# Pairs of 256-column products with stationary tokens, issued as one 512-column matmul per half of the tokens

## The chip, the cores and the metric

The kernel runs on one core of a Trainium2 chip. The metric is the device time of one execution in microseconds: the median of three runs of the kernel before is 1721.67 us (1721.51 to 1723.84).

## The reference, cut to what matters

Two transformer stacks of depth two follow each other on 256 tokens of width 1024. Each layer adds a scale, a shift and a gate from a conditioning vector `c`; the products below are the ones that the change touches.

```python
mod = c_act @ ada_w[i] + ada_b[i]                      # 1024 x 9216 (first stack), 1024 x 6144 (second)
h = modulate(rms_norm(x, ln_ffn1[i]), sh1, sc1)
x = x + 0.5 * g1 * ((silu(h @ wg) * (h @ wu)) @ wd)    # feed-forward, F = 2816
q, k, v = split(h @ w_qkv, 3)                          # attention: q and k are normed by head
z = gelu(h @ w_in); u, v = split(z, 2)                 # spatial gating: v is normed over its columns
q, f_pre, i_in, g = split(hmix @ w_in, ...)            # hgrn2: i_in and g are used with tokens on rows
q, k_c, v_c, k_s, v_s, k_w, v_w, gate = split(h @ w_in, ...)   # nsa: v_s and v_w with tokens on rows
a, v = split(hffn @ w_up, 2)                           # conv_ffn: two of eleven pieces of v
```

## The kernel before, in words

There are ten stages: feed-forward (0, 2, 3, 5), attention (1), spatial gating (4), hgrn2 (6), convolutional feed-forward (7, 9) and nsa (8). Every weight is read from HBM in pieces of 1 MB (tile `raw`, four slots) and split for float32 accuracy: ScalarE writes the rounded part `whi`, VectorE the remainder `wlo = raw - whi`. Both have six slots of 1024 columns, taken in program order. The normed tokens are split in the same way into `hhi` and `hlo`. Each product is three matmuls: hi by hi, hi by lo, lo by hi.

Most products keep the weights stationary (`up_t`, 256 tokens moving). Where a result is wanted with tokens on its rows, `up_x` keeps 128 tokens stationary and moves 256 columns of weights. It is called with two column sets. Each half of the tokens then has two chains of 24 matmuls, one for each set, and a PSUM tile takes both halves of one set. Since a chain writes one tile, its matmuls stay in their order: for k = 0 to 7 hi and lo weights with `hhi`, then eight with `hlo`. The down products (`pd`) have 512 columns moving and tokens stationary.

At the end of a stage, `down_rest` finishes the first half of the tokens and then the second; the residual (`gy`, `x`), the squares, a power on GpSimd, the scaled rows `xs`, eight transposes (`xT`), eight `h` and then `hhi`, `hlo` follow for one half after the other. Meanwhile TensorE has the rest of the down products and what the next stage can already do. Apart from stage 0, each stage begins with an `up_x` block.

The order on each engine is not written by hand. The program hands its instructions to `Plan`, which simulates the engines and picks at each step the ready instruction with the smallest number in program order; a tile without a free slot, or a chain whose operand is late in that simulation, lets others go first. What comes out is a fixed order per engine, and on the chip every engine waits at the head of its list. Background steps (the products for `mod`: a 1 MB load and two VectorE instructions `acc` each) are interleaved by `tick()`, called once for each load of weights.

Of the kernel before, what the change touches and what calls it, by code (L numbers as in the profile page):

```python
# [9 lines left out]
F32 = mybir.dt.float32  # L10
# [523 lines left out]
class Model:  # L534
# [370 lines left out]
    def up_x(self, w, cols, new, name):  # L905
# [17 lines left out]
                self.mms(p[:, h], pairs)  # L923
        return ps

    def down_begin(self, nk):
        self.acc_d = [[self.pd([128, 512], "pd") for n in range(2)] for h in range(2)]
        self.pend, self.nk = [], nk
# [49 lines left out]
    def flip_tokens(self, a):  # L978

        pt = self.pu([128, 2, 2, 128], "aT")  # L980
        for j in range(2):
            for h in range(2):
                self.nc.tensor.transpose(pt[:, j, h], a[:, h, 128 * j:128 * j + 128], self.ident)
        return pt.rearrange("p j h q -> p j (h q)")


# [99 lines left out]
    def ffn(self, wg, wu, wd, end, acts=()):  # L1086
        nc = self.nc
        acts = list(acts)
        if not acts:
            pg, pv = self.up_x([wg, wu], [0, 0], self.pu, "pgv")  # L1090
            sg = self.s([128, 2, 256], "sg")
            nc.scalar.activation(sg, pg, AF.Silu)
            a32 = self.s([128, 2, 256], "a32")
            nc.vector.tensor_tensor(a32, pv, sg, op=OP.mult)
            pt = self.flip_tokens(a32)
            hi, lo = self.m([128, 2, 256], "ahi", F32R), self.m([128, 2, 256], "alo", F32R)
            nc.scalar.activation(hi, pt, AF.Copy)
            nc.vector.tensor_tensor(lo, pt, hi.bitcast(F32), op=OP.subtract)
            acts.append((hi, lo))
        for f in range(len(acts), 11):  # L1100
            pg = self.up_t(wg, 256 * f, self.pu, "pg")
            pv = self.up_t(wu, 256 * f, self.pu, "pv")
            sg = self.s([128, 2, 256], "sg")
            nc.scalar.activation(sg, pg, AF.Silu)
            a32 = self.s([128, 2, 256], "a32")
            nc.vector.tensor_tensor(a32, pv, sg, op=OP.mult)
            acts.append(self.act_pair(a32, [128, 2, 256]))
        self.ffn_down(wd, acts, end)
# [8 lines left out]
    def conv_ffn(self, i, wup, wd, end):  # L1117
        nc = self.nc
        acts = []
        for f in range(11):  # L1120
            if f == 0:
                vx = []
                for px in self.up_x(wup, [F, F + 256], self.pu, "px"):
                    vx.append(self.m([128, 2, 256], "vx"))
                    nc.scalar.activation(vx[-1], px, AF.Copy)
            if f < 2:
                pv = self.flip_tokens(vx[f])
            pa = self.up_t(wup, 256 * f, self.pu, "pa")
            if f >= 2:
                pv = self.up_t(wup, F + 256 * f, self.pu, "pv")  # L1130
            y = self.s([128, 2, 256], "y")
            cw = self.convw[i]
            for j in range(2):
                t = 2 * f + j
                nc.scalar.activation(y[:, j], pa[:, j], AF.Identity, scale=cw[:, 44 + t:45 + t],
                                     bias=self.cols2[:, 22 * i + t:22 * i + t + 1])
                nc.vector.scalar_tensor_tensor(y[:, j, 1:], pa[:, j, :255], cw[:, 22 + t:23 + t], y[:, j, 1:],
                                               op0=OP.mult, op1=OP.add)
                nc.vector.scalar_tensor_tensor(y[:, j, 2:], pa[:, j, :254], cw[:, t:t + 1], y[:, j, 2:],
                                               op0=OP.mult, op1=OP.add)  # L1140
            sg = self.s([128, 2, 256], "sg")
            nc.scalar.activation(sg, y, AF.Silu)
            a32 = self.s([128, 2, 256], "a32")
            nc.vector.tensor_tensor(a32, pv, sg, op=OP.mult)
            acts.append(self.act_pair(a32, [128, 2, 256]))
        self.ffn_down(wd, acts, end)
# [58 lines left out]
    def attention(self, end):  # L1205
        nc, a = self.nc, self.a
        w = a["attn_w_qkv"][0]
        acts = []
        for hp in range(4):
            qk = []  # L1210
            pqk = self.up_x(w, [256 * hp, D + 256 * hp], self.pd, "pqk")
            for i, g in ((0, self.qg8), (1, self.cols2[:, 47:48])):
                p = pqk[i]
                pv = p.rearrange("p a (s d) -> p (a s) d", d=64)
                r = self.seg_rstd(pv, 8, 64, "rqk")
                qn = self.m([128, 2, 256], "qn")
                nc.vector.tensor_tensor(qn.rearrange("p a (s d) -> p (a s) d", d=64), pv,
                                        r[:, :, None].to_broadcast([128, 8, 64]), op=OP.mult)
                pt = self.pu([128, 2, 2, 128], "qkT")
                for h in range(2):  # L1220
                    for t in range(2):
                        nc.tensor.transpose(pt[:, h, t], qn[:, t, 128 * h:128 * h + 128], self.ident)
                qt = self.m([128, 2, 256], "qT")
                nc.scalar.activation(qt, pt.rearrange("p h t q -> p h (t q)"), AF.Copy, scale=g)
                qk.append(qt)
            p, = self.up_x(w, [2 * D + 256 * hp], self.pd, "pv")
            v = self.m([128, 2, 256], "v")
            nc.scalar.activation(v, p, AF.Copy)
            acts.append(self.attend(hp, qk[0], qk[1], v))
        self.down_begin(8)  # L1230
        wo = a["attn_w_o"][0]
        for f in range(4):
            hi, lo = acts[f]
            self.down(wo, 2 * f, [(hi[:, j], lo[:, j]) for j in range(2)], SKEW[self.now])
        end()
# [88 lines left out]
    def sgu(self, end):  # L1324
        nc, a = self.nc, self.a
        w = a["sgu_w_in"][0]
        vt = [self.P.tile([128, D], F32, name="vt", tag="xs") for h in range(2)]
        st = [self.small(16, "vst") for h in range(2)]
        pv = []
        for b in range(4):  # L1330
            if b % 2 == 0:
                pv += self.up_x(w, [D + 256 * b, D + 256 * b + 256], self.pd, "pv")
            p = pv[b]
            for h in range(2):
                nc.scalar.activation(vt[h][:, 256 * b:256 * b + 256], p[:, h], AF.Gelu, accum_out=st[h][:, b:b + 1])
        for h in range(2):
            m = st[h]
            nc.vector.tensor_reduce(m[:, 4:5], m[:, 0:4], axis=AX.X, op=OP.add)
            nc.vector.tensor_scalar(m[:, 5:6], m[:, 4:5], 1.0 / D, None, op0=OP.mult)
            nc.vector.tensor_scalar(m[:, 6:7], m[:, 5:6], -1.0 / 32., None, op0=OP.mult)  # L1340
            ss = self.small(4, "vss")
            junk = self.m([128, 512], "junk")
            for c in range(2):
                nc.scalar.activation(junk, vt[h][:, 512 * c:512 * c + 512], AF.Square, scale=1 / 32.,
                                     bias=m[:, 6:7], accum_out=ss[:, c:c + 1])
            r = self.rstd(ss, 2)
            nc.vector.tensor_scalar(vt[h], vt[h], m[:, 5:6], r, op0=OP.subtract, op1=OP.mult)
# [22 lines left out]
        for f in range(4):  # L1370
            hi, lo = acts[f]
# [36 lines left out]
    def hgrn(self, end):  # L1408
# [1 line left out]
        w = a["hg_w_in_2"][0]  # L1410
        acts = []
        for hp in range(4):
            pi, pg = self.up_x(w, [2 * D + 256 * hp, 3 * D + 256 * hp], self.pd, "pig")
            v = self.m([128, 2, 256], "v")
            nc.scalar.activation(v, pi, AF.Copy)
            sg = self.sigmoid(pg, 1.0, "sg")
            nc.vector.tensor_tensor(sg, pg, sg, op=OP.mult)
            pf = self.up_t(w, D + 256 * hp, self.pd, "pf")
            lf = self.sigmoid(pf, 1.0, "lf")
            kk = self.sigmoid(pf, -1.0, "kk")  # L1420
# [120 lines left out]
    def nsa(self, end):  # L1541
        nc, a = self.nc, self.a
        w = a["nsa_w_in_2"][0]
        vs = []
        for p in self.up_x(w, [D + 256 + 512, D + 256 + 1024], self.pd, "pv"):
            v = self.m([128, 2, 256], "v")
            nc.scalar.activation(v, p, AF.Copy)
            vs.append(v)

        self.kt = [self.P.tile([128, 2, 2, 256], F32, name="kt", tag=t) for t in ("accg", "gb")]  # L1550
        for i in range(2):
# [167 lines left out]
    def nsa_group(self, g, t, q, vs, vc, lct, gv):  # L1719
# [67 lines left out]
        with nc.together():  # L1787

            nc.tensor.matmul(o, vc[:, g].rearrange("n e d -> n (e d)"), lct, start=True, stop=False)
            for i in range(last + 1):  # L1790
                br, k = divmod(i, t + 1)
                for e in range(2):
                    nc.tensor.matmul(o[64 * e:64 * e + 64], vs[br][:, k, es], pts[e][br][:, k], start=False, stop=i == last)
        act = self.m([128, 2, 2, 128], "nact", F32R)
        nc.scalar.activation(act[:, 0], o, AF.Copy)
        nc.vector.tensor_tensor(act[:, 1], o, act[:, 0].bitcast(F32), op=OP.subtract)
# [98 lines left out]
```

## Time and profile before

| | |
|---|---|
| median of three runs | 1721.67 us |
| the profiled execution | 1727.68 us |
| its span | 1725.9 us |
| TensorE matmul busy | 97% of the span |
| VectorE, ScalarE busy | 76%, 55% |
| 16 DMA engines | 71.6% |
| mean granted TensorE clock | 0.992 of full speed |

Busy time of TensorE counts overlapping, pipelined matmuls, so that cadence (start to start) and waits are read instead. All durations below come from the profiled execution, which lies 6.0 us above the median.

### The profile page before, as it was taken

What the parts mean: (1) busy time and instruction counts of PE and PEld (TensorE: products, weight loads), DVE (VectorE), ACT (ScalarE), POOL (GpSimd) and SP (SyncE); (2) the same over time, 40 slices, a digit from 0 to 9 for tenths busy, and PEclk for the clock granted to TensorE, in tenths of its full rate; (3) what the DMA queues carried; (4) which work ended last, traced back from release to release, by engine and by line L of the source; (5) the groups of instructions that cost most, each with busy time, mean ns of one, the idle gap of its engine ahead of it and who ended that gap; (6) DMA issues with size and microseconds to landing.
All of it is one profiled execution on the core that took longest, in us unless ns stands there. A gap on an engine that the chain in (4) does not pass through costs nothing.

```text
span 1725.9 us, 30930 instructions
## 1 busy us (share of the span) xinstructions
PE 1681.5 (97%) x12646; PEld 1512.0 (88%) x12646; DVE 1309.6 (76%) x1950; ACT 948.0 (55%) x1581; POOL 64.4 (4%) x60
## 2 busy tenths in 40 slices
PE   7999999999999999999999999999999999999998
PEld 5899779889988999788999879989998887589986
DVE  4778688886777888677877787889897557878754
ACT  4444366654445544364644368877554556766542
POOL 0000012100001000001000000000000000000000
PEclk9999999999999999999999999999999999999999
DMA  9998875668886998676788865357888565247662
GB/s 297 308 332 308 284 236 192 212 218 282 276 311 220 329 316 304 233 234 229 235 274 302 311 222 175 120 173 236 278 291 304 187 198 217 86 160 231 215 212 73
DMA packets 264208, 415.25 MB, mean 241 GB/s; under 512 B 12811, under 2 KB 210294, under 8 KB 263042
## 3 DMA queue, kind: packets, MB, share of 16 engines
q1 hardware_dynamic: 264065, 413.27, 71.6%
q8 instruction: 99, 1.62, 0.4%
q14 instruction: 44, 0.35, 0.1%
HBM read 412.14 MB, written 1.10 MB: 239 GB/s over the span
## 4 chain that ended last, share of the span: by engine, by line
PE 86%; DMA 5%; DVE 4%; ACT 3%; issue 1%; POOL 1%; SPq 0%; DVEq 0%; POOLq 0%; ACTq 0%
PE pd L514 22%; PE pv L514 21%; PE pg L514 12%; PE pa L514 7%; PE pig L514 3%; PE pgv L514 3%; PE pq L514 3%; PE pqk L514 2%; DMA raw<-in_ffn_wd 2%; PE pf L514 1%; DVE wlo L514 1%; PE px L514 1%; DMA raw<-in_ffn_wu 1%; ACT whi L514 1%; PE ada L514 1%
## 5 line engine op out<-in xcount | busy, mean ns | idle before, releaser
L514 ACT ACTIVATE whi<-raw 128x1024 fp32r<-128x1024 f32 x512 | 534.5, 1056 | 549.1 <-PE pd L514 152.2
L514 DVE TENSOR_TENSOR wlo<-raw,whi 128x1024 fp32r<-128x1024 f32 x512 | 616.5, 1220 | 230.1 <-ACT whi L514 227.1
L514 PE MATMUL pv<-hhi,whi 128*128 128x256 f32 x912 | 257.5, 282 | 0.0
L514 PE MATMUL pv<-hlo,whi 128*128 128x256 f32 x912 | 257.2, 282 | 0.0
L514 PE MATMUL pv<-hhi,wlo 128*128 128x256 f32 x912 | 257.0, 282 | 0.0
L514 DVE SCALAR_TENSOR_TENSOR acc<-raw,csil,acc 128x1024 f32<-128x1024 f32 x192 | 245.8, 1280 | 14.3 <-DMA raw<-in_ada_w 11.7
L514 PE MATMUL pd<-whi,ahi 128*128 128x512 f32 x604 | 239.2, 397 | 0.6 <-ACT ahi L514 0.6
L514 PE MATMUL pd<-wlo,ahi 128*128 128x512 f32 x604 | 237.8, 394 | 0.0
L514 PE MATMUL pd<-whi,alo 128*128 128x512 f32 x604 | 237.4, 394 | 0.0
L514 PE MATMUL pg<-hhi,whi 128*128 128x256 f32 x624 | 176.9, 283 | 0.0
L514 PE MATMUL pg<-hhi,wlo 128*128 128x256 f32 x624 | 176.1, 282 | 0.0
L514 PE MATMUL pg<-hlo,whi 128*128 128x256 f32 x624 | 176.0, 282 | 0.0
L514 PEld LDWEIGHTS pv<-hhi,whi 128*128 128x128 f32 x912 | 174.3, 191 | 1.2 <-issue 1.2
L514 PEld LDWEIGHTS pv<-hhi,wlo 128*128 128x128 f32 x912 | 174.4, 191 | 0.0
L514 PEld LDWEIGHTS pv<-hlo,whi 128*128 128x128 f32 x912 | 174.2, 191 | 0.0
L514 PEld LDWEIGHTS pd<-whi,ahi 128*128 128x128 f32 x604 | 113.7, 188 | 30.8 <-issue 5.3
L514 PEld LDWEIGHTS pd<-whi,alo 128*128 128x128 f32 x604 | 113.7, 188 | 25.4 <-DVE alo L514 0.2
L514 PEld LDWEIGHTS pd<-wlo,ahi 128*128 128x128 f32 x604 | 113.7, 188 | 25.2 <-DVE wlo L514 0.9
L514 PEld LDWEIGHTS pg<-hhi,whi 128*128 128x128 f32 x624 | 119.3, 191 | 2.6 <-issue 2.5
L514 PEld LDWEIGHTS pg<-hhi,wlo 128*128 128x128 f32 x624 | 119.3, 191 | 0.0
L514 PEld LDWEIGHTS pg<-hlo,whi 128*128 128x128 f32 x624 | 119.3, 191 | 0.0
L514 PE MATMUL pa<-hhi,whi 128*128 128x256 f32 x352 | 99.6, 283 | 0.0
(358 smaller groups left out, 3096.0 us busy)
## 6 DMA issues: line engine op xcount, KB each, us to landing
raw<-in_ada_w SPq DMA_DIRECT2D x112, 1024.0 KB
raw<-in_ffn_wd SPq DMA_DIRECT2D x44, 1024.0 KB
raw<-in_ffn_w_up SPq DMA_DIRECT2D x44, 1024.0 KB
raw<-in_ffn_wg SPq DMA_DIRECT2D x42, 1024.0 KB
raw<-in_ffn_wu SPq DMA_DIRECT2D x42, 1024.0 KB
raw<-in_ffn_w_down SPq DMA_DIRECT2D x22, 1024.0 KB
raw<-in_hg_w_in SPq DMA_DIRECT2D x16, 1024.0 KB
raw<-in_attn_w_qkv SPq DMA_DIRECT2D x12, 1024.0 KB
```

The costliest lines, as they stand in the source:

```text
L514: f(*[real(v) for v in args], **{k: real(v) for k, v in kw.items()})
```

## The change

A new function `up_w` takes the place of `up_x` in the sixteen calls that have two column sets; the one call with a single set (attention's v) keeps `up_x`. It loads each set in two pieces of 512 KB, by halves of the contraction, side by side into one `raw` tile, and splits it into four parts of two k each, in which both sets stand side by side. Each half of the tokens has one chain of 24 matmuls of 512 columns and a PSUM tile of its own. `tick()` is called after each of the four loads. The consumers work by halves of the tokens instead of by column sets.

```diff
+    def up_w(self, w, cols, new, name):
+        parts = []
+        for i in range(2):
+            raw = self.P.tile([128, 4, 2, 256], F32, name="raw", tag="raw")
+            for j, c0 in enumerate(cols):
+                v = w[j] if isinstance(w, list) else w
+                self.load(raw[:, :, j], v[512 * i:512 * i + 512, c0:c0 + 256].rearrange("(k p) f -> p k f", p=128))
+                self.tick()
+            parts += [self.split(raw[:, 2 * k:2 * k + 2], [128, 2, 2, 256]) for k in range(2)]
+        ps = [None, None]
+        for h in self.halves:
+            hs = slice(128 * h, 128 * h + 128)
+            ps[h] = new([128, 2, 256], name)
+            pairs = []
+            for k in range(8):
+                hi, lo = parts[k // 2]
+                pairs += [(self.hhi[:, k, hs], hi[:, k % 2]), (self.hhi[:, k, hs], lo[:, k % 2])]
+            for k in range(8):
+                pairs.append((self.hlo[:, k, hs], parts[k // 2][0][:, k % 2]))
+            self.mms(ps[h], pairs)
+        return ps
...
-            pg, pv = self.up_x([wg, wu], [0, 0], self.pu, "pgv")
+            ps = self.up_w([wg, wu], [0, 0], self.pu, "pgv")
             sg = self.s([128, 2, 256], "sg")
-            nc.scalar.activation(sg, pg, AF.Silu)
             a32 = self.s([128, 2, 256], "a32")
-            nc.vector.tensor_tensor(a32, pv, sg, op=OP.mult)
-            pt = self.flip_tokens(a32)
+            for h in self.halves:
+                nc.scalar.activation(sg[:, h], ps[h][:, 0], AF.Silu)
+                nc.vector.tensor_tensor(a32[:, h], ps[h][:, 1], sg[:, h], op=OP.mult)
+            pt = self.flip_tokens([a32[:, h] for h in range(2)])
...
-            pi, pg = self.up_x(w, [2 * D + 256 * hp, 3 * D + 256 * hp], self.pd, "pig")
+            pig = self.up_w(w, [2 * D + 256 * hp, 3 * D + 256 * hp], self.pd, "pig")
```

The other calls change alike: attention norms q and k of one half together, spatial gating has four GELU instructions of 512 columns in place of eight of 256, and convolution and nsa copy by halves.

How the order moves is shown at the entry into stage 6, where the block is named `pig`. On TensorE, these rows lead up to the second half's transposes, before the change:

```order
L514 MATMUL pig<-whi,hhi 128x256
L514 MATMUL pig<-wlo,hhi 128x256
L514 MATMUL pig<-whi,hhi 128x256
L514 MATMUL pig<-wlo,hhi 128x256
L514 MATMUL pig<-whi,hhi 128x256
L514 MATMUL pig<-wlo,hhi 128x256
L514 MATMUL pig<-whi,hhi 128x256
L514 MATMUL pig<-wlo,hhi 128x256
L514 MATMUL pig<-whi,hlo 128x256 x7
L514 MATMUL xT<-ident,xs 128x128 x4
L514 MATMUL pig<-whi,hlo 128x256
L514 MATMUL xT<-ident,xs 128x128 x4
```

And this is all that stands between the transposes of the first and the second half after the change:

```order
L514 MATMUL xT<-ident,xs 128x128 x8
L514 MATMUL pig<-whi,hhi 128x512
L514 MATMUL pig<-wlo,hhi 128x512
L514 MATMUL pig<-whi,hhi 128x512
L514 MATMUL pig<-wlo,hhi 128x512
L514 MATMUL pig<-whi,hhi 128x512
L514 MATMUL pig<-wlo,hhi 128x512
L514 MATMUL pig<-whi,hhi 128x512
L514 MATMUL pig<-wlo,hhi 128x512
L514 MATMUL pig<-whi,hhi 128x512
L514 MATMUL xT<-ident,xs 128x128 x8
```

Before, 47 of 96 matmuls stand ahead of the second half's transposes (the same rows go on upwards to the first half's eight `xT`); after, 9 of 48.

On VectorE at the same place, from the first half's last `hlo` on, before the change (`ss`, `x_99` and `xs` are the second half's norm):

```order
L514 TENSOR_TENSOR hlo<-h_10715,hhi 128x4x128
L514 TENSOR_TENSOR xrow<-x_99,raw 128x512
L514 TENSOR_SCALAR ss_10686<-ss_10686 128x1
L514 TENSOR_TENSOR wlo<-raw,whi 128x1024
L514 TENSOR_SCALAR ss_10686<-ss_10686 128x1
L514 SCALAR_TENSOR_TENSOR ss_10686<-ss_10686 128x1
L514 TENSOR_SCALAR x_99<-xrow,ss_10686 128x512 x2
L514 TENSOR_SCALAR xs<-xrow,ss_10686 128x512
L514 TENSOR_TENSOR wlo<-raw,whi 128x1024
L514 CAST hhi<-h_10808 128x2x128
```

And after it:

```order
L514 TENSOR_TENSOR hlo<-h_10307,hhi 128x4x128
L514 TENSOR_SCALAR ss_10269<-ss_10269 128x1 x2
L514 SCALAR_TENSOR_TENSOR ss_10269<-ss_10269 128x1
L514 TENSOR_SCALAR x_99<-xrow,ss_10269 128x512
L514 TENSOR_SCALAR xs<-xrow,ss_10269 128x512
L514 TENSOR_SCALAR x_99<-xrow,ss_10269 128x512
L514 TENSOR_TENSOR wlo<-raw,whi 128x1024 x2
L514 CAST hhi<-h_10358 128x2x128 x2
```

The first `wlo` of the piece before is the block's fourth part; the two of the piece after are its third and fourth, and both stand behind `xs`.

On ScalarE near the end of stage 5, `sums` releases the transposes `modt`, for which TensorE waits. Before (`dhi` are parts of the ninth of eleven loads of the down weights, the two `whi` behind it of the tenth):

```order
L514 ACTIVATE whi<-raw 128x1024 x9
L514 ACTIVATE dhi<-raw 128x512 x4
L514 ACTIVATE whi<-raw 128x1024 x2
L514 ACTIVATE sums<-modc 128x512
L514 ACTIVATE whi<-raw 128x1024 x4
```

After:

```order
L514 ACTIVATE whi<-raw 128x1024 x8
L514 ACTIVATE dhi<-raw 128x512 x2
L514 ACTIVATE sums<-modc 128x512
L514 ACTIVATE dhi<-raw 128x512 x2
L514 ACTIVATE whi<-raw 128x1024 x6
```

`sums` moved from behind the tenth load to the middle of the ninth, and `modc`, which it reads, from behind 192 matmuls of `pd` to behind 144.

## Rows read from the trace of the kernel before

**Rows 1.** The page: span and busy time of the engines
```profile
span 1725.9 us, 30930 instructions
PE 1681.5 (97%) x12646; PEld 1512.0 (88%) x12646; DVE 1309.6 (76%) x1950; ACT 948.0 (55%) x1581; POOL 64.4 (4%) x60
```
**Rows 2.** Chain of waits in order of time (start, us, what): runs of matmuls
```profile
359.90 8.40 PE pgv L514 x70
...
679.55 44.09 PE pd L514 x192
...
755.81 16.68 PE pv L514 x139
...
1177.72 9.35 PE px L514 x78
...
1673.88 38.96 PE pd L514 x168
```
**Rows 3.** Waits of TensorE: who for whom, us in total, times, longest
```profile
PE xT L514 <- DVE xs L514: 9.2, 4, 5.2
PE modt L514 <- ACT sums L514: 3.0, 2, 2.7
...
PE abp L514 <- DMA hankel<-bdram: 2.7, 1, 2.7
```
**Rows 4.** Timeline of the entry into stage 6 (start, us, engine, instruction)
```profile
1022.53 1.03 PE L514 MATMUL xT<-ident,xs 128*128 128x128 f32 x8
...
1027.59 1.21 DVE L514 TENSOR_TENSOR wlo<-raw,whi 128x1024 fp32r<-128x1024 f32 x1
...
1028.18 0.19 ACT L514 ACTIVATION_READ_ACCUMULATOR xs<-xrow 128x1 f32 x1
...
1029.24 0.89 DVE L514 TENSOR_SCALAR x<-xrow,ss 128x512 f32<-128x512 f32 x2
...
1030.04 0.48 DVE L514 TENSOR_SCALAR xs<-xrow,ss 128x512 f32<-128x512 f32 x1
1030.16 0.71 ACT L514 ACTIVATE xs<-xrow,ss 128x512 f32<-128x512 f32 x1
...
1030.60 0.63 PE L514 MATMUL xT<-ident,xs 128*128 128x128 f32 x4
```
**Rows 5.** Chain of waits: last runs of the block at three entries
```profile
557.56 5.01 PE pgv L514 x40
...
832.87 4.75 PE pgv L514 x40
...
1033.58 5.02 PE pig L514 x40
```
**Rows 6.** Timeline of TensorE: first transpose at four other entries
```profile
352.56 0.30 PE L514 MATMUL xT<-ident,xs 128*128 128x128 f32 x1 [2.55 <-DVE xs L514]
...
546.51 0.27 PE L514 MATMUL xT<-ident,xs 128*128 128x128 f32 x1
...
821.70 0.27 PE L514 MATMUL xT<-ident,xs 128*128 128x128 f32 x1
...
1170.75 0.30 PE L514 MATMUL xT<-ident,xs 128*128 128x128 f32 x1 [1.27 <-DVE xs L514]
```
**Rows 7.** The page's costliest groups: VectorE's background step
```profile
L514 DVE SCALAR_TENSOR_TENSOR acc<-raw,csil,acc 128x1024 f32<-128x1024 f32 x192 | 245.8, 1280 | 14.3 <-DMA raw<-in_ada_w 11.7
```
**Rows 8.** Stretches: PE, PEld, DVE, ACT, POOL busy; PEclk, DMA share, GB/s
```profile
225.00:250.00 25.00, 21.55 (x157) 18.61 (x155) 21.95 (x33) 17.17 (x33) 6.57 (x3) 1.00 0.75 236
350.00:375.00 25.00, 21.67 (x172) 21.46 (x172) 20.86 (x33) 17.96 (x35) 1.43 (x2) 0.93 0.51 170
1000.00:1025.00 25.00, 21.70 (x99) 16.69 (x96) 19.68 (x32) 15.02 (x29) 2.02 (x2) 0.93 0.67 215
```
**Rows 9.** Timeline near the end of stage 5
```profile
1002.68 2.00 ACT L514 ACTIVATE whi<-raw 128x1024 fp32r<-128x1024 f32 x2 [2.11 <-DMA raw<-in_ffn_wd]
...
1005.23 0.66 PE L514 MATMUL modt<-ident,sums 128*128 128x128 f32 x4 [2.70 <-ACT sums L514]
```

More of the change, by code (lines that the diff above doesn't have):

```diff
@@ L982, in flip_tokens @@
             for h in range(2):
-                self.nc.tensor.transpose(pt[:, j, h], a[:, h, 128 * j:128 * j + 128], self.ident)
+                self.nc.tensor.transpose(pt[:, j, h], a[h][:, 128 * j:128 * j + 128], self.ident)
         return pt.rearrange("p j h q -> p j (h q)")
@@ L1121, in conv_ffn @@
             if f == 0:
[L1122 to L1125, printed above, removed]
+                px = self.up_w(wup, [F, F + 256], self.pu, "px")
+                vx = [self.m([128, 2, 256], "vx") for h in range(2)]
+                for h in self.halves:
+                    nc.scalar.activation(vx[h], px[h], AF.Copy)
             if f < 2:
-                pv = self.flip_tokens(vx[f])
+                pv = self.flip_tokens([vx[h][:, f] for h in range(2)])
             pa = self.up_t(wup, 256 * f, self.pu, "pa")
@@ L1209, in attention @@
         for hp in range(4):
+            pqk = self.up_w(w, [256 * hp, D + 256 * hp], self.pd, "pqk")
+            qn = [None, None]
+            for t in self.halves:
+                pv = pqk[t].rearrange("p a (s d) -> p (a s) d", d=64)
+                r = self.seg_rstd(pv, 8, 64, "rqk")
+                qn[t] = self.m([128, 2, 256], "qn")
+                nc.vector.tensor_tensor(qn[t].rearrange("p a (s d) -> p (a s) d", d=64), pv,
+                                        r[:, :, None].to_broadcast([128, 8, 64]), op=OP.mult)
             qk = []
-            pqk = self.up_x(w, [256 * hp, D + 256 * hp], self.pd, "pqk")
             for i, g in ((0, self.qg8), (1, self.cols2[:, 47:48])):
[L1213 to L1218, printed above, removed]
                 pt = self.pu([128, 2, 2, 128], "qkT")
-                for h in range(2):
-                    for t in range(2):
-                        nc.tensor.transpose(pt[:, h, t], qn[:, t, 128 * h:128 * h + 128], self.ident)
+                for t in self.halves:
+                    for h in range(2):
+                        nc.tensor.transpose(pt[:, h, t], qn[t][:, i, 128 * h:128 * h + 128], self.ident)
                 qt = self.m([128, 2, 256], "qT")
@@ L1328, in sgu @@
         st = [self.small(16, "vst") for h in range(2)]
[L1329 to L1335, printed above, removed]
+        for b in range(2):
+            pv = self.up_w(w, [D + 512 * b, D + 512 * b + 256], self.pd, "pv")
+            for h in self.halves:
+                nc.scalar.activation(vt[h][:, 512 * b:512 * b + 512], pv[h].rearrange("p a f -> p (a f)"), AF.Gelu,
+                                     accum_out=st[h][:, b:b + 1])
         for h in range(2):
             m = st[h]
-            nc.vector.tensor_reduce(m[:, 4:5], m[:, 0:4], axis=AX.X, op=OP.add)
+            nc.vector.tensor_tensor(m[:, 4:5], m[:, 0:1], m[:, 1:2], op=OP.add)
             nc.vector.tensor_scalar(m[:, 5:6], m[:, 4:5], 1.0 / D, None, op0=OP.mult)
@@ L1412, in hgrn @@
         for hp in range(4):
-            pi, pg = self.up_x(w, [2 * D + 256 * hp, 3 * D + 256 * hp], self.pd, "pig")
+            pig = self.up_w(w, [2 * D + 256 * hp, 3 * D + 256 * hp], self.pd, "pig")
             v = self.m([128, 2, 256], "v")
-            nc.scalar.activation(v, pi, AF.Copy)
-            sg = self.sigmoid(pg, 1.0, "sg")
-            nc.vector.tensor_tensor(sg, pg, sg, op=OP.mult)
+            sg = self.m([128, 2, 256], "sg")
+            for h in self.halves:
+                nc.scalar.activation(v[:, h], pig[h][:, 0], AF.Copy)
+                nc.scalar.activation(sg[:, h], pig[h][:, 1], AF.Sigmoid)
+                nc.vector.tensor_tensor(sg[:, h], pig[h][:, 1], sg[:, h], op=OP.mult)
             pf = self.up_t(w, D + 256 * hp, self.pd, "pf")
@@ L1543, in nsa @@
         w = a["nsa_w_in_2"][0]
[L1544 to L1548, printed above, removed]
+        vs = [self.m([128, 2, 256], "v") for h in range(2)]
+        pv = self.up_w(w, [D + 256 + 512, D + 256 + 1024], self.pd, "pv")
+        for h in self.halves:
+            nc.scalar.activation(vs[h], pv[h], AF.Copy)
         self.kt = [self.P.tile([128, 2, 2, 256], F32, name="kt", tag=t) for t in ("accg", "gb")]
@@ L1792, in nsa_group @@
                 for e in range(2):
-                    nc.tensor.matmul(o[64 * e:64 * e + 64], vs[br][:, k, es], pts[e][br][:, k], start=False, stop=i == last)
+                    nc.tensor.matmul(o[64 * e:64 * e + 64], vs[k][:, br, es], pts[e][br][:, k], start=False, stop=i == last)
         act = self.m([128, 2, 2, 128], "nact", F32R)
```

## The prediction

> **What bounds the kernel now.** I read the page first: TensorE 97% busy with matmuls, VectorE 76%, ScalarE 55% [rows 1]. That share counts overlapping matmuls, so I went to the chain of waits for the cadence, then to TensorE's waits for where it stands idle, then to the timeline of the stage entries. In the chain the reader is to see long unbroken runs of TensorE [rows 2], and in the waits few and short ones: 9.2 us for the scaled rows `xs` at four entries, 3.0 us for `sums`, 2.7 us for one load in attention [rows 3]. So TensorE's list sets the time nearly throughout, and what matters is (a) what one matmul of the list costs and (b) whether the head of the list is ready. The change alters both.
>
> **The cadence.** Blocks of `up_x` run 70 matmuls of 256 columns in 8.40 us, 139 in 16.68 and 78 in 9.35: 287 in 34.43, 120.0 ns each. The down products have the same shape as the new matmul (tokens stationary, 512 columns of split weights moving): 192 in 44.09 and 168 in 38.96, 360 in 83.05, 230.7 ns each [rows 2]. Two of the first cost 240.0 ns, one of the second 230.7: 9.3 ns less. A block falls from 96 to 48 matmuls, so it gains 48 x 9.3 ns = 0.45 us; sixteen blocks gain 7.1 us. The bound on the one side is this, on the other nothing, where the block isn't what its stage waits for.
>
> These rows have 13 ns over 256 columns at 2.4 GHz and 17 ns over 512. The Trainium skill (TensorE: Matmul & The Clock Gate, section Back-to-back issue gap) gives a fixed 2.5 ns for each matmul at any width; a pair would then gain 2.5 ns and the sixteen blocks 1.9 us, an estimate from that page, and my sum would come out 5.2 us later. The measured runs disagree and decide.
>
> **What the block now waits for.** Seven blocks lie inside a stage (three each in attention and hgrn2, one in spatial gating), with other products around them; I take their whole gain: 7 x 0.45 = 3.1 us less. Nine open a stage, and there the order matters. At the end of a stage the down products hold four of six `whi` and `wlo` slots, so two of the block's four parts are split early and two during the norm. Before, the first two are a whole column set: a chain of 24 matmuls, 2.9 us, can run on the first half of the tokens with them alone, and on the second half again. After, the first two are k = 0 to 3 of both sets, and the one chain stops after 8 of 24 (1.8 us); the tenth matmul needs the third part's `wlo`, the fourteenth the fourth part's.
>
> Worked out at the entry into stage 6: the first transposes start at 1022.53, the squares of the second half are read by 1028.37, `xs` ends 2.15 us later on VectorE and 2.50 us later on ScalarE, at 1030.52 and 1030.87 [rows 4]. After, one `whi` less (1.1 us by its neighbours) lies between the first half's `h` and those squares: 1027.3, so `xs` is there at 1029.4 and 1029.8, and the second half's transposes are over at 1030.5. Behind `xs`, VectorE has one `x` (half of 0.89) and then both parts, 1.21 us each [rows 4]: the third is ready at 1031.1, the fourth at 1032.3. The 9 matmuls ahead of those transposes are over by about 1026.6, so TensorE stands for nearly 3 us, then again for the third and fourth part. At 1032.3 there are 13 of 48 matmuls done; 35 x 230.7 ns = 8.1 us bring the block's end to 1040.4. Before, it ends at 1033.58 + 5.02 = 1038.60 [rows 5], with one matmul of `pf` inside. That is 1.8 + 0.1 = 1.9 us later, in place of 0.45 us earlier.
>
> I counted the other entries alike, by the order after and the durations above, from the first transpose [rows 6] to the block's end:
> - Stage 2: between `xs` and the fourth part VectorE has an `acc` (1.28 us [rows 7]), the third part and all of the second half's `hhi` and `hlo`. The fourth part comes 13.0 us after 352.56, 22 matmuls (5.1 us) follow: 18.1 us against 15.7 (368.30 [rows 2]), with two matmuls of `pg` inside; 0.7 us comes back, since one `gy` less stands ahead of the first `xs`, for which TensorE waits 2.55 us there [rows 6]. Together 1.5 us later.
> - Stage 3: the third part before `xs`, the fourth right behind it, 9.2 us after 546.51; 35 matmuls: 17.3 us against 16.1 (562.57 [rows 5]), of which one matmul is another product's. 1.3 us later.
> - Stage 5: both parts behind `xs` and two `acc` more on VectorE's way; the fourth part at 10.0, the end at 18.1 against 15.9 (837.62 [rows 5]). With the first transposes a little late too, 2.4 us later.
> - Stage 7: fourth part at 9.2, end at 17.3 against 16.3 (1187.07 [rows 2]); 0.7 us comes back as in stage 2 (the wait is 1.27 us [rows 6]). 0.2 us later.
> - Stages 1, 4, 8 and 9 have the third part ahead of `hhi`, or other matmuls for the gap. I take 1.2 us gained of their 1.8.
>
> The nine entries together: 1.9 + 1.5 + 1.3 + 2.4 + 0.2 - 1.2 = 6.1 us later, their gain in cadence already inside. With the blocks inside stages: 6.1 - 3.1 = 3.0 us later.
>
> **The clock.** After long idle stretches the granted clock falls to 1.2 GHz for a while: the stretches from 350 and from 1000 us have a mean of 0.93, with waits of 2.55 and 2.70 us in them; that from 225 us has a wait of as long for `hankel` and stays at 1.00 [rows 3, 6, 8, 9]. A mean of 0.93 over 25 us is 0.07 x 25 = 1.75 us of work lost. New idle stretches of 2 to 3 us at stages 2, 5 and 6 put one more such fall on the path, or two; I take one: 1.8 us.
>
> **The rest.** The 512 KB loads are 32 more issues on SP, which has no row in TensorE's waits; with nothing to hide them in they'd be some 0.4 us each. Two more ticks per block bring the background loads forward and end them earlier in each stage: same bytes, same VectorE work. ScalarE and VectorE have a few more, smaller instructions in feed-forward and hgrn2, four fewer GELU in spatial gating; these lie beside matmuls. One place can go either way: `modt` in stage 5. TensorE waits 2.70 us for `sums`, which stands behind a load that came late [rows 9]. After, `sums` needs only the ninth load, not the tenth; but TensorE asks for it 48 matmuls (11.1 us) earlier. Gone with the fall of the clock behind it, this is 4.5 us gained; if the loads come as late as now, it is about as much lost, an estimate. In attention the stall for `hankel` (2.7 us [rows 3]) has 23 + 12 matmuls before it now in place of 25, so up to 2.7 us less, or the same if a background load is put in front of it. I take nothing for both and keep both ends: 7 us down, 5 us up.
>
> Sum: 3.0 + 1.8 = 4.8 us later than the profiled execution's 1727.68 us. That one lies 6.0 us over the median of the runs, and I shift by that: 1721.67 + 4.8 = 1726.5 us.
>
> **Rivals.**
> - The gain stands (faster). If VectorE and ScalarE have the late parts ready before the transposes, all sixteen blocks gain: 1721.67 - 7.1 = 1714.6; with the stall at `modt` gone too, 1710. For it: the long even runs of [rows 2], and PSUM tiles that come free by halves. Against: the order itself, which puts the parts behind `xs` at stages 5, 6 and 7.
> - Gain and loss cancel (no change). The entries lose less, because idle time there was partly spent before (9.2 us for `xs` [rows 3]): entries 3 us later, inside blocks 3 us earlier: 1721.7.
> - The background sums decide (slower by more). `sums` stands behind late loads at the end of stage 5, TensorE stands 6 us in place of 2.7 and falls to the low clock: 4 to 5 us on top of the forecast, 1731. It decides from the point where the ninth load lands later than TensorE's 144th down matmul.
> - The change isn't what it says: no, the list has 48 matmuls of 512 columns a block.
>
> **How the numbers follow.** My forecast has 0.42, the background rival 0.18, no net change 0.20, the full gain 0.20. Its own range is 1724 to 1730. For eight in ten: downwards I stop between the full gain and the forecast's lower end, at 1714.5; upwards at 1735, the background rival with a second fall of the clock. About 0.2%, 3.4 us, is what a measurement of this kernel tells from no change: slower by more takes the forecast and the background rival, 0.58, less what lies near the border, plus a little of the cancelling case: 0.56. Within it 0.23, faster 0.21.
>
> **What would show it.** Right: 230 ns from matmul to matmul inside the blocks; TensorE's waits with `pig`, `pgv` for `wlo`, and `xT` for `xs` longer by several us in all; blocks at stages 2, 3, 5 and 6 that end 17 to 18 us after the first transpose; more stretches below a clock of 1.00 after them. Wrong: those blocks end within 16 us, or the cadence is the gain and the waits are those of before. Then the slot argument fails, or ScalarE and VectorE are faster through the entry than I counted.

## The result, and the profile after

| | before | after |
|---|---|---|
| median | 1722.76 us (4 runs, 1721.51 to 1724.76) | 1733.03 us (4 runs, 1731.33 to 1734.65) |
| ratio, 95% interval | | 1.0051 [1.0036, 1.0066] |
| the profiled execution | 1727.68 us | 1731.33 us |

The change is slower by 0.5%, 6 to 11 us. The prediction had the direction, and 1733.0 lies in its wide range (1714.5 to 1735); but it had about half of the size (1726.5), and the measured time lies above the range of its own forecast (1724 to 1730). The two profiled executions differ by only 3.7 us, because the first trace of before is one of its longer executions; a second trace of before (below) is the better pair.

The page of after has the span and the engines, to lay beside [rows 1]; there are 768 fewer matmuls (16 blocks of 96 became 48), and 8.6 us less of their busy time:

```profile
span 1729.6 us, 29460 instructions
PE 1672.9 (97%) x11878; PEld 1463.5 (85%) x11878; DVE 1310.7 (76%) x1957; ACT 953.3 (55%) x1588; POOL 62.9 (4%) x60
```

The chain of waits of after (start, us, what) has runs inside two blocks and one of the down products:

```profile
1306.06 33.13 PE pd L514 x144
...
1375.41 7.76 PE pv L514 x34
...
1537.38 7.60 PE px L514 x33
```

Inside the blocks a matmul of 512 columns comes every (7.76 + 7.60) / 67 = 229.3 ns. That is the cadence foretold from [rows 2] (230.7). The waits of TensorE in after (us in total, times, longest), to lay beside [rows 3]:

```profile
PE xT L514 <- DVE xs L514: 16.5, 10, 5.1
PE pTc L514 <- DVE lc L514: 6.3, 1, 6.3
PE pgv L514 <- DVE wlo L514: 3.2, 2, 2.0
...
PE abp L514 <- DMA hankel<-bdram: 0.8, 1, 0.8
```

`xs` costs 7.3 us more than in [rows 3], and `pgv` waits 3.2 us for `wlo` where the trace of before has 0.5, as foretold. `modt` is gone. New, and in no part of the prediction, is one wait of 6.3 us in nsa: the transposes `pTc` wait for `lc`, the scores of its compressed branch. The timeline there (start, us, engine, instruction):

```profile
1447.59 1.52 PE L514 MATMUL pcs<-kct,q 128*128 128x32 f32 x12
...
1449.79 3.71 DVE L514 TENSOR_TENSOR wlo<-raw,whi 128x1024 fp32r<-128x1024 f32 x3
1450.07 1.99 ACT L514 ACTIVATE whi<-raw 128x1024 fp32r<-128x1024 f32 x2
...
1452.08 1.28 ACT L514 ACT_TABLE_LOAD   x1
...
1453.88 0.29 ACT L514 ACTIVATE lc<-lc 128x128 f32<-128x128 f32 x1
...
1455.40 1.01 PE L514 MATMUL pTc<-ident,lc 128*32 128x128 f32 x4 [6.29 <-DVE lc L514]
```

`pcs` ends at 1449.1, the exponent of `lc` starts at 1453.88: ScalarE first splits two weights and loads a table, VectorE splits three. The stretches around it (PE, PEld, DVE, ACT, POOL busy; PEclk, DMA share, GB/s) show what follows:

```profile
1028.00:1031.00 3.00, 2.88 (x11) 2.11 (x9) 2.97 (x5) 3.00 (x9) 0.00 (x0) 0.52 0.02 7
1444.00:1451.00 7.00, 5.11 (x41) 3.10 (x39) 5.38 (x19) 4.32 (x8) 0.00 (x0) 1.00 1.02 407
1452.00:1468.00 16.00, 12.60 (x45) 5.48 (x46) 8.41 (x27) 8.45 (x26) 0.00 (x0) 0.50 0.48 172
```

From 1452 on, while TensorE still waits, it has 1.2 GHz, for 16 us. The first of these rows is the other fall, behind the entry into stage 6, where the forecast had put it. That entry, in the timeline of after, to lay beside [rows 4]:

```profile
1021.09 1.03 PE L514 MATMUL xT<-ident,xs 128*128 128x128 f32 x8
...
1024.92 0.40 PE L514 MATMUL pig<-whi,hhi 128*128 128x512 f32 x1
...
1026.92 0.49 DVE L514 TENSOR_SCALAR xs<-xrow,ss 128x512 f32<-128x512 f32 x1
...
1027.46 1.41 PE L514 MATMUL xT<-ident,xs 128*128 128x128 f32 x8 [2.14 <-DVE xs L514]
...
1027.72 2.35 DVE L514 TENSOR_TENSOR wlo<-raw,whi 128x1024 fp32r<-128x1024 f32 x2
...
1028.99 0.80 PE L514 MATMUL pig<-wlo,hhi 128*128 128x512 f32 x1
...
1037.39 2.00 PE L514 MATMUL pig<-whi,hlo 128*128 128x512 f32 x8
```

TensorE stops behind the ninth matmul (1024.92) and waits for `xs`; the two late `wlo` stand behind `xs` on VectorE, and the tenth matmul starts at 1028.99. All as foretold.

### The profile page after: what moved, and what is told of

Its sections match the earlier page's. It is cut to its first block, busy times and chain, and to the rows that moved or that the text cites. A ratio compares the mean times of both kernels' runs of the same rounds, so it can differ in the third digit from the quotient of the medians.

```text
span 1729.6 us, 29460 instructions
## 1 busy us (share of the span) xinstructions
PE 1672.9 (97%) x11878; PEld 1463.5 (85%) x11878; DVE 1310.7 (76%) x1957; ACT 953.3 (55%) x1588; POOL 62.9 (4%) x60
## 5 line engine op out<-in xcount | busy, mean ns | idle before, releaser
L514 DVE SCALAR_TENSOR_TENSOR acc<-raw,csil,acc 128x1024 f32<-128x1024 f32 x192 | 246.0, 1281 | 19.9 <-DMA raw<-in_ada_w 17.1
```

Of the source, the lines that this page charges most:

```text
L514: f(*[real(v) for v in args], **{k: real(v) for k, v in kw.items()})
```

## The experiments

Every kernel is made from the two shown above; the diffs are shortened to the lines that matter, and the first one has its condition written out for one stage. A block that opens a stage is called an opener. "After" and "before" are the changed kernel and the one before it. Medians, ratios and intervals are against before in the same batch (1722.66, 1723.09 and 1723.31 us).

**A second trace of before.**

> The kernel before, unchanged, for a second trace of it: which waits of the first trace are of the order, and which of one execution. With an order that is the same there, the run with the block only inside stages took 195.0 us for stage 5 (200.8 in the first trace) and 155.5 for stage 8 (160.2), each counted from first xT to first xT. If the wait of modt for sums and the two low-clock stretches in stage 8 belong to one execution, this one takes some 195 and 156 us there and the whole 1718 to 1723; if they belong to the order, 200 and 160 again and 1727.

1719.85 us. Without any edit, stage 5 takes 196.5 us (200.8 in the first trace, counted from first `xT` to first `xT`), stage 8 157.1 (160.2); the other stages agree within 0.3. Two stretches, of the second trace, and behind them one of the first for the later place:

```profile
1000.00:1025.00 25.00, 23.90 (x132) 19.55 (x125) 22.27 (x39) 18.53 (x36) 4.02 (x4) 1.00 0.58 179
1500.00:1515.00 15.00, 13.27 (x66) 8.95 (x66) 11.93 (x30) 9.27 (x23) 0.55 (x1) 1.00 0.09 24
```

```profile
1505.00:1520.00 15.00, 13.27 (x52) 8.02 (x52) 9.24 (x25) 7.44 (x21) 0.55 (x1) 0.77 0.00 1
```

So the 2.70 us for `sums` and the fall behind it in [rows 8, 9], and the second fall in stage 8, belong to that execution: 4.3 + 3.1 = 7.4 of the 7.8 us between the two.

Against the second trace, after is 11.5 us longer (spans 1729.6 and 1718.1). Both are short executions of their kernels, 3.5 and 1.7 us under the medians. By stages, worked out from the timelines in the same way (us; "ticks alone" and "two ticks in nsa" are kernels below, "inner" the block inside stages alone, with two ticks):

| stage | before, 2nd | after | two ticks in nsa | ticks alone | inner |
|---|---|---|---|---|---|
| 0 | 216.5 | 217.2 | 217.0 | 216.9 | 217.4 |
| 1 attention | 127.4 | 126.8 | 127.2 | 129.1 | 123.1 |
| 2 | 194.0 | 196.1 | 196.1 | 194.4 | 194.1 |
| 3 | 195.1 | 196.4 | 196.4 | 196.9 | 195.9 |
| 4 spatial gating | 80.1 | 79.7 | 79.7 | 80.3 | 79.8 |
| 5 | 196.5 | 196.8 | 196.7 | 197.8 | 195.8 |
| 6 hgrn2 | 148.3 | 150.9 | 150.9 | 150.0 | 148.5 |
| 7 | 195.1 | 195.5 | 195.5 | 195.8 | 193.8 |
| 8 nsa | 157.1 | 161.9 | 155.8 | 158.5 | 155.4 |
| 9 | 199.8 | 200.2 | 200.6 | 199.7 | 199.9 |

**The block inside stages only.** Attention's and hgrn2's hp = 1 to 3 and spatial gating's second pair call `up_w`, the nine openers keep `up_x` and their consumers.

```diff
+            if hp:
                 pqk = self.up_w(w, [256 * hp, D + 256 * hp], self.pd, "pqk")
+            else:
+                pqk = self.up_x(w, [256 * hp, D + 256 * hp], self.pd, "pqk")
```

> The 512-column block stands only in the seven places inside a stage (three in attention, three in hgrn2, one in spatial gating); the nine blocks that open a stage are those of the kernel before, with their consumers. My theory (cadence gains in every block, the entries give it back and more): 7 x 0.45 = 3.1 us less than before, about 1719.6 where before is 1722.8; waits of xT for xs at stage entries as before (9 us), inner blocks at 230 ns a matmul. Rival A (the loss comes from the four calls of tick and the smaller loads wherever the block stands): 1723 to 1727, no gain, with new waits inside attention or hgrn2. Rival B (cadence isn't a gain on the path): 1722.8.

1717.67 us, 0.9975 [0.9964, 0.9986]: 2.4 to 6.2 us less, which holds the theory's 3.1. So the loss comes with the changed openers; whether by their 512 columns or by their ticks this run doesn't tell.

**The block at the openers only**, the mirror image.

> The mirror image: the 512-column block stands only in the nine places that open a stage, the seven inside a stage are those of the kernel before. Theory: the whole loss and none of the inner gain, 3.1 us over the changed kernel: about 1736, 13 us over before. xT waits 16 us for xs, as in the changed kernel. Rival A (loss spread over all sixteen blocks): between before and the changed kernel, about 1728. Rival B (the inner blocks do not matter): 1733.

1729.47 us, 1.0047 [1.0035, 1.0059]. The 1736 of the theory is missed, and TensorE waits 12.2 us for `xs`, not 16. By the time rival A (1728) is nearest; by the ratios (1.0047, and 1.0051 for after) rival B is: with the openers changed, the inner blocks no longer gain anything. In the traces they still give 0.9 us in hgrn2 and 1.0 in spatial gating, but attention is 3.1 us longer with them and their ticks (126.8 against 123.7).

**Two ticks instead of four.**

```diff
-                self.tick()
+                if j:
+                    self.tick()
```

> The changed kernel with tick called once per raw tile, so twice per block as before, not four times. In the order this puts the third and fourth part's wlo ahead of the second half's xs on VectorE at stages 2 and 7, the third part's at stages 3 and 5, and leaves stages 4, 6, 8 and 9 as they are. Theory (late parts behind xs make the loss, and at these stages the extra background steps push them there): stages 2, 3, 5 and 7 end their blocks 1 to 2 us earlier each, together 5 us less than the changed kernel, about 1728; stage 6 shows the same wait as in the changed kernel. Rival (only the layout by halves of the contraction matters, ticks are nothing): 1733, the same. Third (background work moved later into the stages meets the ends of the stages): 1735 and a wait of modt for sums at the end of stage 5.

1719.39 us, 0.9984 [0.9974, 0.9994]. This one line takes away the whole loss (13.6 us by the medians, 11.5 by the two ratios), far more than I expected, and turns the change into a small gain. The 16.5 us for `xs` and 6.3 for `lc` become:

```profile
PE xT L514 <- DVE xs L514: 11.7, 8, 5.1
...
PE pgv L514 <- DVE wlo L514: 1.9, 2, 1.0
```

`pTc` has no wait any more. The ticks, which the prediction had at nothing, are the suspect.

**The ticks alone, in the kernel before.** Same 256-column chains and loads, one line more:

```diff
             raw = self.w_cols(w[i] if isinstance(w, list) else w, c0, 256)
+            if len(cols) == 2:
+                self.tick()
```

> The kernel before (256-column chains, same loads and parts) with one change: tick is called twice after each load of a block with two column sets, so four times per block as in the changed kernel. In the order this alone puts the late parts' wlo behind xs at the entries into stages 2, 3, 5, 6 and 7, and takes the four background products ada from between pcs and pTc in nsa. Theory as it stands after the run with two ticks (the ticks make the loss, not the 512-column layout): nsa 5 to 6 us longer with a wait of pTc for lc of 6 us, entries 1 us each, 1730 to 1736. Rival (layout by halves of the contraction and the slots make the loss; ticks matter only with them): 1722 to 1725 outside nsa, at most 1728 with it.

1728.38 us, 1.0027 [1.0013, 1.0040], slower by 2.2 to 6.9: between the theory's 1730 and the rival's 1728, so that the time alone decides nothing, and about half of what after loses (1.0051). Its trace has the waits of after without the new block:

```profile
PE xT L514 <- DVE xs L514: 13.5, 6, 5.0
PE pTc L514 <- DVE lc L514: 4.9, 1, 4.9
```

In nsa the theory misses: the wait is there, but the stage is only 1.4 us longer than in the second trace of before, not 5 to 6.

What the entries do, worked out from the timelines: us from the first transpose to the end of the block (start of its last matmul plus the cadence), and in brackets TensorE's wait ahead of that transpose.

| entry | foretold | before, 2nd | after | ticks alone | two ticks |
|---|---|---|---|---|---|
| 1 | | 17.5 | 18.2 | 18.6 | 18.3 |
| 2 | 18.1 | 15.6 (2.6) | 17.5 (0.6) | 15.9 (3.6) | 15.7 (1.3) |
| 3 | 17.3 | 15.9 | 17.2 | 17.8 | 15.8 |
| 4 | | 19.4 | 19.3 | 19.6 | 19.2 |
| 5 | 18.1 | 15.7 | 17.1 | 16.5 | 16.2 |
| 6 | 17.9 | 15.9 | 18.1 | 16.6 | 18.6 |
| 7 | 17.3 | 16.2 (1.3) | 16.3 (2.2) | 16.5 (2.2) | 14.3 (1.3) |
| 8 | | 15.1 | 15.5 | 15.9 | 15.3 |
| 9 | | 15.1 | 15.4 | 15.1 | 15.5 |

With the brackets, after loses 7 us against before at the nine entries, the ticks alone 8, the new block with two ticks 1. A tick brings a background step forward, and its two `acc` of 1.28 us [rows 7] stand on VectorE just where `gy`, `xs` and the late `wlo` queue. At the entry into stage 5 VectorE has this around the second half's `xs`, in the second trace of before:

```profile
826.33 1.22 DVE L514 TENSOR_TENSOR wlo<-raw,whi 128x1024 fp32r<-128x1024 f32 x1
827.99 0.49 DVE L514 TENSOR_SCALAR xs<-x,ss 128x512 f32<-128x512 f32 x1 [0.44 <-POOL ss L514]
828.39 1.28 DVE L514 SCALAR_TENSOR_TENSOR acc<-raw,csil,acc 128x1024 f32<-128x1024 f32 x1
...
830.59 1.22 DVE L514 TENSOR_TENSOR wlo<-raw,whi 128x1024 fp32r<-128x1024 f32 x1
```

And this with the ticks alone, where `acc` has taken the place of a `wlo` ahead of `xs` (after has the same three instructions, from 828.71):

```profile
830.08 1.28 DVE L514 SCALAR_TENSOR_TENSOR acc<-raw,csil,acc 128x1024 f32<-128x1024 f32 x1
831.80 0.49 DVE L514 TENSOR_SCALAR xs<-x,ss 128x512 f32<-128x512 f32 x1 [0.44 <-POOL ss L514]
832.20 2.36 DVE L514 TENSOR_TENSOR wlo<-raw,whi 128x1024 fp32r<-128x1024 f32 x2
```

The ticks aren't all of it: stage 6, which has no background steps of its own, is late by the block itself (18.6 with two ticks).

**Two ticks in nsa only**, the rest as in after:

```diff
-                self.tick()
+                if j or self.now != 8:
+                    self.tick()
```

> The changed kernel with two ticks instead of four in the one block of nsa (stage 8), four everywhere else; layout as changed. In the order the four ada products stand between pcs and pTc again. Theory (half of the loss is this one place: a wait of 6.3 us for lc and 17 us at the low clock instead of 7): stage 8 takes 157 us instead of 161.9, the whole about 1727 to 1728; entries at stages 2, 3, 5, 6 and 7 as in the changed kernel. Rival A (the nsa wait is hidden or comes back later): 1732 to 1733. Rival B (nsa is the whole loss): 1720.

1727.49 us, 1.0020 [1.0007, 1.0033]; stage 8 takes 155.8 us, the entries are those of after. The same place in its timeline:

```profile
1448.13 2.77 PE L514 MATMUL pcs<-kct,q 128*128 128x32 f32 x12
...
1450.82 1.94 PE L514 MATMUL ada<-raw,csil 128*32 128x512 f32 x8
...
1451.27 0.31 ACT L514 ACTIVATE lc<-lc 128x128 f32<-128x128 f32 x1 [1.97 <-DVE lc L514]
...
1452.81 1.01 PE L514 MATMUL pTc<-ident,lc 128*32 128x128 f32 x4
```

Eight background products `ada` fill TensorE between `pcs` and `pTc`, and `lc` goes ahead of the splits. With four ticks the `ada` loads are issued earlier in the stage, their products are done, and weights stand there ready to be split instead. In this trace the low clock is over soon (again PE, PEld, DVE, ACT, POOL; PEclk):

```profile
1449.00:1454.00 5.00, 4.95 (x23) 2.65 (x25) 2.90 (x15) 3.03 (x13) 0.00 (x0) 0.50 0.87 341
1455.00:1471.00 16.00, 16.00 (x121) 12.87 (x121) 10.50 (x28) 9.12 (x23) 0.00 (x0) 1.00 0.32 122
```

The second trace of before has this short fall too:

```profile
1443.00:1449.00 6.00, 5.95 (x21) 1.96 (x20) 4.09 (x18) 4.69 (x12) 0.00 (x0) 0.50 0.98 366
```

So 5.5 us of the loss by the medians (6.1 in the stage) hang on one block's two ticks.

**Other slots for the late parts.** The opener's third and fourth part become eight tiles of 512 columns in the pool of 22 that the activations use:

```diff
+            if i and early:
+                for k in range(4):
+                    hi, lo = self.m([128, 2, 256], "dhi", F32R), self.m([128, 2, 256], "dlo", F32R)
+                    self.split_to(hi, lo, raw[:, k])
```

> The changed kernel with the third and fourth part of each block that opens a stage taken from another pool (eight tiles of 512 columns, 22 slots) in place of the whi and wlo slots that the down products hold; the rest is as changed. In the order 21 of 24 matmuls of the first half stand ahead of the second half's transposes at stage 5 in place of 9, 15 in place of 9 at stages 3 and 6, 10 in place of 9 at stage 2. Theory (slots hold the late parts back): stage 5 gains 2 us, stages 3 and 6 one us each, stage 2 under a half; less 0.2 us for each entry for more, smaller split instructions; 1729 to 1731. Rival (the slots are not what the parts wait for, VectorE and ScalarE are full there): 1733 or later, TensorE's wait for xs as long as in the changed kernel (16 us).

1720.43 us, 0.9995 [0.9982, 1.0008]: more than expected, and not only where expected. Stage 5's block ends at 14.9 (17.1), stage 6's at 16.2 (18.1), stage 2's at 15.7 (17.5), but stage 3's at 18.2 (17.2), at the low clock; attention and nsa are 3 us shorter each, which the theory had not (another order in both; `pTc` still waits 4.9 us). The slots do hold the late parts back, at three of the four entries that were named; how much of the gain is theirs this run doesn't tell.

**Both.**

> The changed kernel with both edits: late parts of each opening block in the other pool, and two ticks per block. Theory 1 (slots and ticks act on the same wait, the parts behind xs): no better than two ticks alone, 1718 to 1720. Theory 2 (they add): 1715 to 1717. The small splits of 512 columns cost some 0.2 us per entry of VectorE and ScalarE, so 1721 is possible where that lies on the path.

1715.54 us, 0.9951 [0.9937, 0.9965]: more than either alone, as theory 2 has it. If they added in full, 0.9984 less the 0.0056 that the slots gave with four ticks would be 0.9928, an estimate with an interval of its own; they add in good part.

**And the chain in another order.**

```diff
-            for k in range(8):
-                pairs += [(self.hhi[:, k, hs], hi), (self.hhi[:, k, hs], lo)]
-            for k in range(8):
-                pairs.append((self.hlo[:, k, hs], part[k][0]))
+            for q in (0, 4):
+                for k in range(q, q + 4): ...     # hhi by hi, hhi by lo
+                for k in range(q, q + 4): ...     # hlo by hi
```

> The changed kernel with early slots and two ticks, and the chain in another order: hi by hi, hi by lo and lo by hi of k = 0 to 3, then of k = 4 to 7, so that 12 of 24 matmuls need only the two early parts, not 8. Theory (the chain stops where a late part is wanted): stages 2, 6 and 7, where the block still waits, end 0.5 to 1 us earlier; 1713.5 to 1715. Rival (hlo comes later than hhi, so that asking for it earlier costs what the parts give): 1715.5 to 1718.

1713.31 us, 0.9941 [0.9918, 0.9963]; the interval holds the last kernel's ratio, so this stays open. Of the places named one bears the theory out, stage 6, which ends its block at 15.2 (15.9 without); stages 2 and 7 don't, at 16.5 and 15.8 (16.5 and 15.5).

**The price of the cadence by itself.** In before, each 512-column matmul of the down products becomes two:

```diff
+            for c in (slice(0, 256), slice(256, 512)):
+                o = self.acc_d[h][n][:, c]
-                nc.tensor.matmul(o, ah, hi, start=f == 0, stop=False)
+                nc.tensor.matmul(o, ah, hi[:, c], start=f == 0 and c.start == 0, stop=False)
```

> The kernel before with each 512-column matmul of the down products (1872 of them; those of nsa are left as they are) issued as two of 256 columns, same weights, same sums: the price of the cadence by itself, with a lever 39 times that of one block. By the rows (120.0 and 230.7 ns) 1872 x 9.3 ns = 17.4 us more, about 1740. By a fixed gap of 2.5 ns for each matmul 4.7 us more, 1727.4. A cadence that is hidden by other work at these places: 1722.7.

1731.52 us, 1.0041 [1.0029, 1.0054]: 5.0 to 9.3 us, half of the 17.4. Two runs of the down products in its chain:

```profile
1308.53 44.32 PE pd L514 x375
...
1674.38 40.03 PE pd L514 x336
```

711 in 84.35 us are 118.6 ns each, not 120.0: a pair gives 237.3, 6.6 ns over the 230.7 of [rows 2], and 1872 x 6.6 ns = 12.3 us. The last third doesn't show: stage 5, with 264 more matmuls, takes 196.6 us for 196.5, stage 2, with as many, 196.4 for 194.0. That stages which wait anyway take it up is my reading, not shown. The Trainium skill (TensorE: Matmul & The Clock Gate, section Back-to-back issue gap) has a fixed 2.5 ns over the columns, for matmuls by themselves; in a stream in which each matmul has its weight load, as here, both set the spacing, it says. With the 2.5 ns it would be 1872 x 2.5 ns = 4.7 us, an estimate from that page, just below the interval. The trace agrees with it as little as with my 9.3.

**Inside stages only, two ticks.**

> The 512-column block in the seven places inside a stage only, with two ticks instead of four. Theory (inside a stage the ticks cost nothing, since other products are there to run; the gain is cadence): same as with four ticks, 1717 to 1719, within 2 us. Rival (part of its gain of 5 us came from the background work that the ticks bring forward): 1719.5 to 1722.

1713.78 us, 0.9938 [0.9916, 0.9960]: 3.9 us under the same kernel with four ticks. The theory (ticks cost nothing inside) fails, and so does the rival, which had the sign the other way. Without their extra ticks the seven blocks gain 6.9 to 14.5 us, more than twice the 3.1 of the cadence; what the rest is, this run doesn't tell. Attention takes 123.1 us here, 129.0 there (127.4 in the second trace of before). The two stretches of it that fell to a low clock with four ticks, and the same two with two:

```profile
225.00:250.00 25.00, 22.66 (x153) 19.72 (x152) 21.71 (x33) 17.86 (x35) 6.66 (x3) 0.93 0.68 223
275.00:300.00 25.00, 22.40 (x126) 17.91 (x125) 22.84 (x50) 14.40 (x33) 4.38 (x2) 0.93 0.71 233
```

```profile
225.00:250.00 25.00, 22.11 (x159) 19.04 (x157) 22.49 (x33) 18.23 (x36) 6.61 (x3) 1.00 0.76 243
275.00:300.00 25.00, 24.25 (x155) 20.73 (x154) 22.04 (x50) 17.27 (x37) 6.84 (x3) 1.00 0.61 199
```

Two means of 0.93 over 25 us are 3.5 of the 5.9 us at most, and one trace of each doesn't tell whether the ticks brought the falls.

**The same with early slots for the 256-column openers** (the second set's parts as eight small tiles).

> 512-column blocks inside the stages (two ticks); the nine opening blocks keep 256 columns, but the second set's four parts lie in the other pool, so that they do not wait for the slots of the down products. Theory (entries are ruled by late parts, whichever width): entries at stages 2, 5, 6 and 7 end up to 1 us earlier than in the kernel before, 1714 to 1717. Rival (the opening block with 256 columns had its parts in time already): 1718, as with the inner blocks alone.

1711.72 us, 0.9928 [0.9906, 0.9951], the lowest median of all, 0.7% under before and 1.2% under after. Stages 2, 3, 5 and 6 end their blocks at 14.7, 14.8, 15.1 and 15.5, all earlier than before; stage 7 at 16.0. The entry into attention, which the theory didn't name, ends at 20.2 instead of 17.5, and attention takes 126.4 us (123.1 in the kernel above). Against the kernel above it is 2 us, and the intervals overlap.

## Why the prediction was right, and where not

- **Cadence.** 229.3 ns in the blocks: right. That all of it shows in the time: not shown. Taken by itself the pair's price was 6.6 ns, and 8.4 of 12.3 us reached the end.
- **Seven inner blocks, 3.1 us less.** The number is right when they stand alone with their four ticks (2.4 to 6.2), but by luck: with two they give 6.9 to 14.5, so that the cadence isn't all that they gain, and the ticks take part of it back. In after nothing is left of it: by the ratios the openers alone cost as much as the whole change (1.0047 and 1.0051), and attention is longer with the inner blocks and their ticks.
- **Nine entries.** Foretold 6.1 us later, and 1.8 for the clock; measured 7, with the clock inside. That the sums are near is luck in part, since the single terms miss on both sides. With the waits in brackets stage 6 is 2.2 later (1.9 foretold), stage 3 1.3 (1.3), stage 5 1.4 (2.4), stage 7 1.0 (0.2), and stage 2, foretold 1.5 later, is as before. By the blocks' ends stages 3 and 6 came out within 0.2 us of the forecast, stage 2 within 0.6, stage 5 at 17.1 for 18.1. At stage 6 `xs` and the fourth part came a little earlier than counted (6.3 and 9.0 us behind the first transpose, for 6.9 and 9.8), and what that saved went into the low clock from 1028. At stage 2 the wait ahead of the first transpose fell by 1.9, not 0.7. Stage 7 ended at 16.3 for 17.3, but its wait grew from 1.27 to 2.22 where I had 0.7 coming back. "I take 1.2 us gained" for stages 1, 4, 8 and 9 was wrong: they lost 1.3.
- **Why the parts are late.** The step that failed: "Two more ticks per block bring the background loads forward and end them earlier in each stage: same bytes, same VectorE work", taken at nothing. I read the late `wlo` out of the order after and put them down to the four of six slots. The ticks alone, with the old block, make the same entries late by 8 us; the new block with two ticks loses 1. Same work, but earlier, in front of a norm, is not the same. The slots were no error, but not the whole cause: they matter with two ticks (1715.5 against 1719.4), and with four they took the loss away as well (1720.4 against 1733.0). By the times the ticks alone are about half of the loss (1.0027 against 1.0051); how ticks, slots and the wide block share the rest is open.
- **Clock, 1.8 us.** The fall behind the entry into stage 6 came as foretold (0.52 from 1028 to 1031). But in after's trace the fall at stage 2 is gone, so the entries have no more of them than before. Nor does a fall always cost its 1.75 us: behind the entry into stage 7 the first trace of before has 0.51 from 1173 to 1176 and the second 1.00 at the same place, and the block ends 16.2 us after the first transpose in both.
- **nsa.** Not foretold at all, and the other half of the loss: 4.8 us longer than in the second trace of before, 6.1 longer than with two ticks. I had put stage 8 among the entries that gain, and looked no further into the stage than its block. This is what separates 4.8 from the measured 10.3: without it the change stands at 1.0020, 1.2 to 5.7 us. Of the 11.5 us between the traces, 7 lie at the entries, 4.4 in nsa behind its entry, and about nothing in all else, where the forecast had the 3.1 of the inner blocks to gain.
- **`modt` and `hankel`, nothing.** Right for `modt`, for a reason I hadn't: its 2.70 us were of one execution (0.7 in the second trace). `hankel` went from 1.9 in the second trace to 0.8.
- **Rivals.** The background did decide, but not at `sums` in stage 5, where I had it; it did so at the entries and in nsa. A gain as large as that of the full-gain rival exists (1711.7), but not as it had it: with two ticks, other slots, and the wide block kept out of the openers.

## What to carry to other kernels

Where a scheduler interleaves background work by a counter, an edit that calls the counter more often moves that work, and must be costed as a move: list for each stage what it now stands in front of, to the stage's end and not only at the edited block. Change width and pacing in separate steps. A wider operand needs more of its parts at once, so put it where its parts are ready (inside a stage), or give an opener's parts slots of their own: with two ticks the kernels that do so came out at 1711.7 to 1715.5.

## What the runs showed of the hardware

- The same matmul of 256 columns came every 120.0 ns in one kind of block and every 118.6 in the halved down products, so a pair's price against 230.7 was 9.3 or 6.6 ns; a price that rests on the difference of two cadences should be measured at the place.
- From about the same place of the same order, 15 us had a granted clock of 0.77 in one execution of before, with 52 instructions of TensorE in them, and 1.00 in another, with 66. A fall of the clock can't be put down to an edit from one trace.
- A fall need not lengthen anything. Behind the entry into stage 7 TensorE is busy 3.00 of 3 us at a clock of 0.51 in one trace of before and 2.24 at 1.00 in the other, and the block ends at the same time: the slower matmuls fill time in which it would have waited.
- In nsa the clock was at 1.2 GHz from 1452, within the 6.3 us wait, to 1468; in the kernel where `ada` filled that gap, it was full again from 1455 on. How much of the 6.1 us is wait and how much clock was not tried apart.
